# A hybrid decoder layer on eight cores: a build-time list scheduler for every engine, GpSimd arithmetic on VectorE, GLU gates ahead of values

## The chip, the cores and the metric

The kernel runs on one Trainium2 chip, on all 8 of its cores (two dies, cores 0 to 3 and 4 to 7). Each core takes half of one prompt (1024 tokens and 128 tokens of history) and four of the 32 sample tokens; no core talks to another. The time is device time of the slowest core, in microseconds (us). Each run lists every core's span and the mean TensorE clock that it was granted. In some executions a die is slow, at a lower clock; such runs are called slow and are not used for verdicts. A milder form stays inside runs called fast: two cores of a die have a clock that is about 0.02 lower and are some 10 to 25 us longer.

Engines: PE is TensorE (PEld its weight loads), DVE is VectorE, ACT is ScalarE, POOL is GpSimd, SP only issues transfers. POOL issues transfers too. Each engine is given one list of instructions; what it means that a list is worked through in order shows in e1, where VectorE stood 32.87 us before one copy.

## The reference, cut to what matters

```python
h = rms_norm(x, norm_mix_g)
z = h @ w_in                       # q | k | v | GLU value | GLU gate
q = rope(rms_norm(q, q_norm_g), pos);  k = rope(rms_norm(k, k_norm_g), pos)
a = attn_prompt(q, k, v, sinks)    # band of 128 keys; attn_sample reads cache_k, cache_v
u = u_val * jax.nn.sigmoid(u_gate)
c, new_c = causal_dwconv(u, c_buf, conv_w, conv_b)         # 31 taps per channel
c = jax.nn.silu(layer_norm(c, conv_ln_g, conv_ln_b))
x = x + jnp.concatenate([a, c], axis=-1) @ w_out
hm = rms_norm(x, norm_mlp_g)
x = x + jnp.square(jax.nn.relu(hm @ w_up)) @ w_down
```

Width 2048, 16 query heads and 4 key heads of 64, 1024 convolution channels, MLP width 8192. Besides `x`, the new keys, values and convolution rows are outputs; most of the sample caches' new content is a shifted copy of the old.

## The kernel before: the parts that matter

The program is first recorded as a list of instructions with their reads and writes, which gives each its dependencies, and then replayed: each engine runs *its own list in the order in which it was recorded*, waiting on semaphores.

```python
def add(self, eng, fn, reads=(), writes=(), key=None, ...):
    ...                      # dependencies from the bytes read and written
    for bk in banks:         # one more rule: engines that touch a PSUM bank keep their order
        for e2, it in self.bank_last[bk].items():
            if e2 != eng:
                ins.deps.add(it)
    self.streams[eng].append(ins)
```

Stage one loads x in 16 chunks, scales each to bf16 on VectorE, squares it on ScalarE, sums the squares on GpSimd, and multiplies by the K/V weights:

```python
for kc in range(16):
    xd.append(dma("sp", xs_(), R(xt_d[kc]), ...))           # four buffers
    dma("pool", WKV(kc), ..., after=[xd[kc - 3]] if kc >= 3 else [])
    ...                                                     # small tables at kc 5 and 8
    ts("dve", HT(kc), xs_(), G1(kc), ALU.mult)
    act(SQX[kc % 2](), xs_(), AF.Square)                    # at kc 0 into SS1
    if kc >= 2:
        tt("pool", SS1(), SS1(), SQX[(kc - 1) % 2](), ALU.add)
    ...                                                     # K/V matmuls of 7 tiles
for kc in range(16):
    dma("pool", WQ(kc), ..., after=[xd[15]] if kc >= 2 else [xd[13]])
```

The norm and rotary of Q and K go through ScalarE, VectorE and GpSimd.

```python
def qk_chain(accv, nh, nt, GC, GS, tix, B_, out_bf, ...):
    act(B_.SQ(hs), accv(hs), AF.Square)                     # reads the PSUM bank
    tt("dve", A(hs), accv(hs), bc(GC(tix)), ALU.mult)       # same bank
    ...                                                     # two half-head products into B
    red(ss(hs), B_.SQ(hs))
    act(rs(hs), ss(hs), AF.Ln, ...); act(rs(hs), rs(hs), AF.Exp, scale=-0.5)
    tt("pool", A(hs), A(hs), B_.B(hs), ALU.add)
    tt("pool", out_bf, A(hs), rsb, ALU.mult)
```

After Q come cache copies and loads, then GLU, convolution and attention interleaved by hand. The convolution needs u shifted by partitions, 16 small SP copies per channel block (`u_done`). After the last block the program reloads x (`xt_load`) and starts the output projection.

```python
dma("sp", R(nks[:, 0:127, :]), R(ck[:, 1:128, :]), "d2d", ...)   # and nvs, ncs: DRAM to DRAM
dma("pool", KTS(...), R(ckt), "cks", ...)                        # old keys, old values
dma("pool", CVB(p=(0, 127)), R(cv...), "cks", ...)
...
for pi in range(3):
    for gate in (True, False):
        u_job(c, pi, wg if gate else wv, gate)
...
def down_group(g, wd, last):          # MLP, after up_group(g + 1)
    for dc in range(16):
        ...
        tt("dve", x3(), accb((0, 3), (0, PW)), x3(), ALU.add)
```

Names: WKV, WQ, wu, wo, wup and wdn are the weights of K/V, Q, the GLU, the output projection and the MLP's two halves; ckt and cv are the old keys and values of the sample caches; nks, nvs and ncs are the new caches; u is the output of the GLU.

Of the kernel before, what the change touches and what calls it, by code (L numbers as in the profile page):

```python
# [31 lines left out]
NO = 1028  # L32
# [8 lines left out]
NKV1 = 7  # L41
# [6 lines left out]
class Ins:  # L48
    __slots__ = ("eng", "fn", "deps", "inc", "count", "key", "is_dma", "group", "name")

    def __init__(self, eng, fn, name=""):
        self.eng = eng
        self.fn = fn
        self.deps = set()
        self.inc = False
        self.count = 0
        self.key = None
        self.is_dma = False
        self.group = False
        self.name = name  # L60

# [88 lines left out]
class Prog:  # L150
    ENGS = ["pe", "act", "dve", "pool", "sp"]

    def __init__(self):
        self.streams = {e: [] for e in self.ENGS}
        self.spaces = {"sb": Space(), "ps": Space()}
        self.finals = []
        self.keycount = {}
        self.bank_last = {}
        self.n = 0

    def add(self, eng, fn, reads=(), writes=(), key=None, group=False, final=False, name="", after=(), claim=()):
# [34 lines left out]
        for ref in claim:  # L196
            for (sp, a, b) in ref.rngs:
                for st in self.spaces[sp].segs(a, b):
                    st[0] = ins
                    st[1] = []  # L200
        if key is not None:
            ins.is_dma = True
            ins.key = key
            ins.group = group
            self.keycount[key] = self.keycount.get(key, 0) + 16
            ins.count = self.keycount[key]
            ins.inc = True
# [4 lines left out]
        return ins  # L212

# [82 lines left out]
def build_program():  # L296
# [138 lines left out]

    def dma(eng, out, in_, key, group=False, final=False, after=()):
        return P.add(eng, lambda e: e.dma_start(out=out.ap, in_=in_.ap), reads=[in_], writes=[out],  # L437
                     key=key, group=group, final=final, after=after)

    def act(out, in_, func, bias=0.0, scale=1.0):  # L440
        rd = [in_]
        b = bias
        s = scale
        if isinstance(bias, Ref):
            rd.append(bias)
            b = bias.ap
        if isinstance(scale, Ref):
            rd.append(scale)
            s = scale.ap
        return P.add("act", lambda e: e.activation(out=out.ap, in_=in_.ap, func=func, bias=b, scale=s),  # L450
                     reads=rd, writes=[out])

    def tt(eng, out, in0, in1, op):
        return P.add(eng, lambda e: e.tensor_tensor(out=out.ap, in0=in0.ap, in1=in1.ap, op=op),  # L454
                     reads=[in0, in1], writes=[out])

    def ts(eng, out, in0, s1, op0, s2=None, op1=None):
# [5 lines left out]
        if isinstance(s2, Ref):  # L463
# [4 lines left out]
                     reads=rd, writes=[out])  # L468

    def cp(eng, out, in_):  # L470
        if eng == "act":
            return P.add("act", lambda e: e.copy(out=out.ap, in_=in_.ap), reads=[in_], writes=[out])  # L472
        return P.add(eng, lambda e: e.tensor_copy(out=out.ap, in_=in_.ap), reads=[in_], writes=[out])  # L473

    def red(out, in_):
        return P.add("dve", lambda e: e.tensor_reduce(out=out.ap, in_=in_.ap, axis=AX.X, op=ALU.add),  # L476
                     reads=[in_], writes=[out])

    def memset(eng, out, val):
        return P.add(eng, lambda e: e.memset(out.ap, val), writes=[out])  # L480

    def mm(out, lhsT, rhs, start, stop):
        return P.add("pe", lambda e: e.matmul(out.ap, lhsT.ap, rhs.ap, start=start, stop=stop),  # L483
                     reads=[lhsT, rhs], writes=[out])

    def tr(out, in_, ident):
        return P.add("pe", lambda e: e.transpose(out.ap, in_.ap, ident.ap), reads=[in_, ident], writes=[out])  # L487
# [34 lines left out]
    for kc in range(16):  # L522
        xs_ = XST[kc % 4]
        xd.append(dma("sp", xs_(), R(xt_d[kc]), "xst%d" % (kc % 4)))
        dma("pool", WKV(kc), R(wkv_d[kc]), "wkv%d" % kc, after=[xd[kc - 3]] if kc >= 3 else [])
# [10 lines left out]
        if kc >= 2:  # L536
            tt("pool", SS1(), SS1(), SQX[(kc - 1) % 2](), ALU.add)
# [3 lines left out]
    tt("pool", SS1(), SS1(), SQX[1](), ALU.add)  # L541
# [6 lines left out]
    def kv_tile(ti, bk):  # L548
        tn, c0, nt = TT[ti]
        for kc in range(16):  # L550
# [3 lines left out]
    kv_tile(7, 0)  # L554
    ptk = ps_f32(7, 1, (10,))
    for ti, (tn, c0, nt) in enumerate(TT):
# [5 lines left out]
    kv_tile(8, 1)  # L562
    kv_tile(9, 2)
    RB = sb(O_X, F32, (NU,))
    for i, (a, b) in enumerate(PU):
        pb = ps_f32(6 - i, 1, (b - a,))
        mm(pb(), ONF(), SS1((U0 + a, U0 + b)), True, True)
# [3 lines left out]
    cp("pool", IDB(), CST((0, 128)))  # L571
    cp("pool", MOWN(), CST((128, 256)))
    cp("pool", MPRV(), CST((256, 384)))
    cp("pool", MPR0(), CST((384, 512)))
    cp("pool", I4(), CST((512, 544)))
    for (GC, GS, g, gs) in ((GCK, GSK, GK, GKS), (GCQ, GSQ, GQ, GQS)):
        tt("pool", GC(), TABIN(0), bc(g, 1, (128, 10, 64)), ALU.mult)
        tt("pool", GS(), TABIN(1), bc(gs, 1, (128, 10, 64)), ALU.mult)
# [15 lines left out]
    KC = [sb(O_H + 7168 + 1024 * i, F32, (4, 64)) for i in range(2)]  # L594
# [3 lines left out]
    def qk_chain(accv, nh, nt, GC, GS, tix, B_, out_bf, out_f32=None):  # L598
# [14 lines left out]
        tt("pool", A(hs, p=pp), A(hs, p=pp), B_.B(hs, p=pp), ALU.add)  # L613
        rsb = bc(rs(hs, p=pp), 2, (nt, nh, 64))
        if out_f32 is not None:
            tt("pool", out_f32, A(hs, p=pp), rsb, ALU.mult)
            cp("pool", out_bf, out_f32)
        else:
            tt("pool", out_bf, A(hs, p=pp), rsb, ALU.mult)
# [5 lines left out]
    for ti, (tn, c0, nt) in enumerate(TT):  # L625
# [11 lines left out]
        kf = head4(KF_L, nt) if tn == "m7" else (head4(KF_S, nt) if tn == "s" else KC[ti % 2](p=pp))  # L637
        qk_chain(RAW[ti], 4, nt, GCK, GSK, ti, kb_, K2[ti](p=pp), out_f32=kf)

    def fin_k(tis, bk):  # L640
        pt = ps_bf16(bk, (4, 2, 128))
        for i, ti in enumerate(tis):
# [17 lines left out]
    def fin_q(qbuf, ti, c0d, nt):  # L660
        pt = ps_bf16(6 + ti % 2, (8, 128))
        qf = Buf("sb", qbuf.ap.rearrange("p h d -> p (h d)"), qbuf.off, (1024,), 2)
# [18 lines left out]
    for kc in range(16):  # L681
        for i in range(3):
# [11 lines left out]
    for i, ti in enumerate(range(4, 10)):  # L694
        for kc in range(16):
# [27 lines left out]
    GT = [sb(O_H + 4096 + 1440 * i, F32, (360,)) for i in range(2)]  # L723
    SGR = [sb(O_H + 6976 + 1440 * i, F32, (360,)) for i in range(2)]
# [14 lines left out]
    later = []  # L739

    def flush():
        while later:
            later.pop(0)()

    def u_job(c, pi, w, gate):
        a, b = PU[pi]
        n = b - a
        acc = dense_bank(n)
        for kc in range(16):
            mm(acc(), w(kc), HT(kc, (U0 + a, U0 + b)), kc == 0, kc == 15)  # L750
        flush()
        i = gts[0] % 2
        if gate:
            gt, sg = GT[i]((0, n)), SGR[i]((0, n))
            rb = RB((a, b))
# [4 lines left out]
            tt("pool", sg, gt, rb, ALU.mult)  # L760
        else:
            sg = SGR[i]((0, n))
            tt("dve", UB[c % 2]((a, b)), acc(), sg, ALU.mult)
            if pi == 2:
                tt("dve", UF(c), acc((322, 356)), SGR[i]((322, 356)), ALU.mult)
            gts[0] += 1

    def u_done(c):
        ub, u4 = UB[c % 2], U4[c % 2]
        first = None  # L770
        for s in range(4):
            for g in range(4):
# [5 lines left out]
                      key="u4%d" % (c % 2))  # L778
        cw4 = PAR((568 + 32 * c, 600 + 32 * c))
        tt("pool", D4[c % 2](), Ref(I4().ap.unsqueeze(1).unsqueeze(1).broadcast_to([128, 4, 8, 32]), I4().rngs),  # L780
# [8 lines left out]
    def conv_job(c, pi):  # L789
        acc = dense_bank(512)  # L790
        for t in range(8):
# [3 lines left out]
        flush()  # L795
        act(CC(c, (512 * pi, 512 * pi + 512)), acc(), AF.Identity, bias=CB(c))

    def conv_sums(c, eng="pool"):
# [10 lines left out]
    def unit_a(ui):  # L809
        n, gp = units[ui]  # L810
        own_c0 = MC0 + 128 * n
        cs = (gp * 4, gp * 4 + 4)
        for kb in range(2):
# [12 lines left out]
    def unit_b(ui):  # L826
# [3 lines left out]
        psd = ps_f32(5, 1, (4, 128))  # L830
        for kb in range(2):
# [12 lines left out]
        later.append(lambda: tt("dve", AT(cs, (128 * n, 128 * n + 128)), pso(), rec(), ALU.mult))  # L844

    def sample_a():
        ktn = KT((0, 2), (SC0, SC0 + SPC))
        cp("dve", Ref(KTS.ap[:, :, :, 127], KTS().rngs), Ref(ktn.ap.rearrange("p c s -> p s c"), ktn.rngs))
        pss2 = [ps_f32(0, 1, (64,)), ps_f32(1, 1, (64,))]
# [12 lines left out]
    def sample_b():  # L862
        psos = ps_f32(4, 1, (8, SPC))
        psds = ps_f32(5, 1, (8, SPC))
        for s in range(SPC):
# [9 lines left out]
        later.append(lambda: tt("dve", AT((0, 8), (1024, NO)), psos(), RECS(), ALU.mult))  # L875
# [10 lines left out]
    for c in range(8):  # L886
        wg, wv = wu.pop(0), wu.pop(0)
        for pi in range(3):
            for gate in (True, False):
                u_job(c, pi, wg if gate else wv, gate)  # L890
                if c == 0 and pi == 0 and gate:
                    while pend:
                        fin_q(*pend.pop(0))
                if job % 3 == 1 and nu < 16:
                    if nu >= 1:
                        unit_b(nu - 1)
                    unit_a(nu)
                    nu += 1
                if c == 4 and pi == 0 and not gate:
                    sample_a()  # L900
                if c == 4 and pi == 1 and not gate:
                    sample_b()
                job += 1
            if c >= 2 and pi < 2:
                conv_job(c - 2, pi)
                if pi == 1:
# [18 lines left out]
    def wo_half(dc, half, src):  # L925
# [3 lines left out]
        accb = acc3(next_slot())  # L929
        for kc in range(8):  # L930
# [13 lines left out]
    def ln_stats():  # L944
        for pi, (a, b) in enumerate(PM):
            pm, pv = ps_f32(6, 1, (PW,)), ps_f32(7, 1, (PW,))
# [36 lines left out]
    def norm2(dc):  # L983
# [3 lines left out]
        if dc == 0:  # L987
            cp("pool", SS(), sq())
        else:
            tt("pool" if dc < 14 else "dve", SS(), SS(), sq(), ALU.add)  # L990
# [7 lines left out]
    def norm2_end():  # L998
        for pi, (a, b) in enumerate(PM):
            pm = ps_f32(6 + pi % 2, 1, (PW,))  # L1000
# [17 lines left out]
    def up_group(g):  # L1018
        hid = HID[g % 2]
        for fi in range(GFF):  # L1020
            w = upq.pop(0)
            accb = acc3(next_slot())
            for kc in range(16):
# [11 lines left out]
    def down_group(g, wd, last):  # L1035
        hid = HID[g % 2]
        for dc in range(16):
            accb = acc3(next_slot())
            for fi in range(GFF):
# [14 lines left out]

    P.finish()
# [147 lines left out]
```

## Time and profile before

| | before |
|---|---|
| time, median of 6 runs | 1454.25 us (1452.68 to 1463.55) |
| span of the profiled core | 1451.3 us |
| PE busy | 1322.7 us (91%) |
| DVE / ACT / POOL busy | 694.6 / 285.8 / 312.3 us |

The chain of waits that ended last, by engine (part 4 of the page), says that the matter is TensorE:

```profile
PE 81%; DVE 6%; issue 4%; ACT 4%; DMA 2%; POOL 1%; SPq 1%; DVEq 0%; ACTq 0%; POOLq 0%
```

So the question is where PE is not busy. Busy time by stretch; the columns are the stretch and its length, then PE, PEld, DVE, ACT and POOL busy with the number of instructions, the granted clock, the DMA share and GB/s (a packet counts where it starts, so that a short stretch can show a share over 1):

```profile
0.00:62.00 62.00, 33.75 (x116) 11.94 (x117) 48.94 (x23) 21.58 (x20) 51.61 (x35) 0.89 0.83 210
62.00:106.00 44.00, 36.02 (x188) 17.72 (x185) 24.31 (x49) 20.44 (x58) 36.72 (x61) 0.95 0.72 114
106.00:168.00 62.00, 52.38 (x283) 25.22 (x284) 29.81 (x34) 21.18 (x38) 43.66 (x20) 0.91 0.33 63
168.00:371.00 203.00, 171.12 (x1399) 90.42 (x1396) 84.12 (x180) 99.22 (x186) 72.24 (x62) 0.96 0.44 76
371.00:387.00 16.00, 4.89 (x44) 1.81 (x48) 4.87 (x10) 3.01 (x4) 0.00 (x0) 0.62 0.99 188
387.00:550.00 163.00, 153.12 (x1037) 99.31 (x1030) 71.97 (x65) 57.52 (x57) 46.07 (x37) 0.96 0.59 109
550.00:1437.00 887.00, 870.93 (x5957) 580.29 (x5956) 429.16 (x377) 62.84 (x61) 61.99 (x117) 1.00 0.47 79
```

The first number after the length is PE: 28 us idle in stage one, 8 and 10 in the Q stages, 32 in the GLU stage, 11 in the short stretch after 371 us, 10 in the projection, and 16 in the MLP.

The price of GpSimd arithmetic is in the groups by shape (count, busy us, mean ns of one, idle before):

```profile
L454 POOL TENSOR_TENSOR arena<-arena 128x1032 f32<-128x1032 f32 x23 | 54.5, 2377 | 22.1 <-ACT arena L450 17.4 <-PE psum L483 4.7
L454 DVE TENSOR_TENSOR arena<-arena 128x1032 f32<-128x1032 f32 x22 | 26.9, 1229 | 21.6 <-ACT arena L450 20.7 <-DVE arena L454 0.2
```

And from the timeline of stage one (start, duration, instruction, idle before):

```profile
16.17 43.40 DVE L467 TENSOR_SCALAR arena<-arena 128x1160 bf16<-128x1160 f32 x13 [1.02 <-DMA arena<-xt]
17.87 0.82 POOL L437 DMA_DIRECT2D arena<-wkv  x1
18.71 2.64 POOL L454 TENSOR_TENSOR arena<-arena 128x1160 f32<-128x1160 f32 x1
```

Thirteen scalings take 43.40 us, 3.3 us each; the first two of the kernel, with POOL quiet, took 0.82 us. The POOL rows repeat every 3.4 us.

SP's timeline shows when transfers were issued. The last 16 copies of u are issued between 371.20 and 382.07 us, and the reloads of x follow them:

```profile
25.57 20.73 SPq L437 DMA_DIRECT2D arena<-xt  x7
102.55 16.28 SPq L437 DMA_DIRECT2D nks<-ck  x1
371.20 10.87 SPq L776 DMA_DIRECT2D arena<-arena  x16
383.01 14.48 SPq L437 DMA_DIRECT2D arena<-xt  x16
```

### The profile page before, as it was taken

To read this page: it belongs to the slowest core of one execution; us is meant where nothing else is said; L and a number is where in the kernel's file an instruction comes from. 1 tells how busy PE (TensorE), PEld (TensorE's weight loads), DVE (VectorE), ACT (ScalarE), POOL (GpSimd) and SP (SyncE) were. 2 spreads that over 40 slices of the span, in tenths; PEclk is the share of its full clock that TensorE was granted. 3 is DMA by queue.
4 is the path that set the end of the run, shared out by engine and by line. 5 is a ranking of instruction groups with operands and counts; after the bars stand their busy time and mean duration, and the time that the engine had idled before them with its cause. 6 is when DMAs were issued, how large, how long until landed. Compare 5 with 4: busy or idle time off the path is not lost.

```text
span 1451.3 us, 22465 instructions; the slowest of 8 cores (1445.6 to 1451.3 us)
## 1 busy us (share of the span) xinstructions
PE 1322.7 (91%) x9016; PEld 826.8 (57%) x9016; DVE 694.6 (48%) x734; ACT 285.8 (20%) x424; POOL 312.3 (22%) x330
## 2 busy tenths in 40 slices
PE   4779788788699979999999999999999999999996
PEld 1334344444366646666666666666666666666664
DVE  6765343343374322544534535535446345354364
ACT  3253345445233621000010010000100100100000
POOL 7976523333202712010010010110100100101000
PEclk8999899999799999999999999999999999999998
DMA  9764254354875358471562543634715526437209
GB/s 255 144 111 87 12 101 81 60 98 80 195 160 74 44 88 140 65 116 30 88 94 47 94 71 61 102 50 67 117 30 88 88 45 100 66 59 124 44 15 218
DMA packets 57336, 130.96 MB, mean 90 GB/s; under 512 B 19064, under 2 KB 22012, under 8 KB 57212
## 3 DMA queue, kind: packets, MB, share of 16 engines
q0 software_dynamic: 38880, 90.74, 40.5%
q1 hardware_dynamic: 18356, 38.80, 9.9%
q8 instruction: 73, 1.20, 0.3%
q14 instruction: 27, 0.22, 0.1%
HBM read 202.73 MB, written 10.35 MB: 147 GB/s over the span
## 4 chain that ended last, share of the span: by engine, by line
PE 81%; DVE 6%; issue 4%; ACT 4%; DMA 2%; POOL 1%; SPq 1%; DVEq 0%; ACTq 0%; POOLq 0%
PE psum L483 81%; DVE arena L454 4%; ACT arena L450 3%; DVE arena L467 2%; DMA arena<-xt 1%; POOL arena L454 1%; SPq L776 1%; DMA arena<-wup 0%; ACT arena L472 0%; DMA arena<-arena 0%; DVE arena L476 0%; PE psum L487 0%; SPq L437 0%; DVEq L265 0%; DVE arena L473 0%
## 5 line engine op out<-in xcount | busy, mean ns | idle before, releaser
L483 PE MATMUL psum<-arena 128*128 128x344 bf16 (+7 forms) x8924 | 1317.5, 323 | 103.8 <-DVE arena L454 38.1
L483 PEld LDWEIGHTS psum<-arena 128*128 128x128 bf16 (+4 forms) x8924 | 821.1, 99 | 596.8 <-issue 170.9
L454 DVE TENSOR_TENSOR arena<-psum,arena 128x1032 f32<-128x1032 f32 (+7 forms) x408 | 423.0, 1050 | 291.8 <-PE psum L483 264.7
L454 DVE TENSOR_TENSOR arena<-arena 128x1032 bf16<-128x1032 bf16 (+6 forms) x252 | 204.7, 824 | 427.1 <-ACT arena L450 410.3
L450 ACT ACTIVATE arena<-psum 128x512 bf16<-128x512 f32 (+6 forms) x150 | 112.5, 787 | 808.9 <-PE psum L483 797.9
L454 POOL TENSOR_TENSOR arena<-arena 128x1032 f32<-128x1032 f32 (+8 forms) x112 | 191.2, 1719 | 174.6 <-ACT arena L450 145.3
L437 POOL DMA_DIRECT2D arena<-wup x64 | 34.0, 531 | 746.1 <-PE psum L483 746.0
L450 ACT ACTIVATE arena<-arena 128x352 f32<-128x352 f32 (+11 forms) x237 | 148.9, 647 | 219.1 <-DVE arena L454 134.4
L467 DVE TENSOR_SCALAR arena<-arena 128x1160 bf16<-128x1160 f32 (+2 forms) x25 | 49.2, 2006 | 12.4 <-DMA arena<-xt 11.3
L437 POOL DMA_DIRECT2D arena<-wdn x64 | 34.0, 551 | 27.9 <-PE psum L483 25.8
L437 POOL DMA_DIRECT2D arena<-wo x16 | 11.6, 726 | 80.8 <-PE psum L483 80.8
L476 DVE TENSOR_REDUCE arena<-arena 128x4 f32<-128x256 bf16 (+4 forms) x27 | 17.2, 638 | 2.0 <-ACT arena L450 1.1
L450 ACT ACTIVATE arena<-psum,arena 128x512 f32<-128x512 f32 x16 | 11.1, 694 | 31.0 <-PE psum L483 31.0
L487 PE MATMUL psum<-arena 128*128 128x128 bf16 (+1 forms) x92 | 7.2, 220 | 10.9 <-DVE arena L454 5.6
L472 ACT COPY arena<-psum 128x1024 bf16<-128x1024 bf16 (+5 forms) x18 | 13.0, 762 | 15.4 <-PE psum L483 12.7
L487 PEld LDWEIGHTS psum<-arena 128*128 128x128 bf16 (+1 forms) x92 | 5.9, 101 | 13.6 <-issue 11.9
L437 POOL DMA_DIRECT2D arena<-wkv x16 | 12.3, 770 | 0.9 <-POOLq L297 0.9
L437 POOL DMA_DIRECT2D arena<-wu x16 | 9.0, 564 | 0.1
L437 POOL DMA_DIRECT2D arena<-wq x16 | 8.5, 599 | 0.0
L450 ACT ACT_TABLE_LOAD x3 | 3.8, 1283 | 21.2 <-PE psum L483 11.2
L473 DVE COPY arena<-psum 128x512 f32<-128x512 f32 (+1 forms) x8 | 4.7, 621 | 4.2 <-PE psum L483 4.2
L473 POOL CAST arena<-arena 128x256 bf16<-128x256 f32 (+3 forms) x15 | 5.2, 398 | 1.3
(11 smaller groups left out, 11.8 us busy)
## 6 DMA issues: line engine op xcount, KB each, us to landing
arena<-wup POOLq DMA_DIRECT2D x64, 512.0 KB, 6.8
arena<-wdn POOLq DMA_DIRECT2D x64, 512.0 KB, 14.5
arena<-xt SPq DMA_DIRECT2D x16, 580.0 KB, 7.7
arena<-arena SPq DMA_DIRECT2D x128, 65.8 KB, 4.5
arena<-xt SPq DMA_DIRECT2D x16, 516.0 KB, 13.6
yt<-arena SPq DMA_DIRECT2D x16, 514.0 KB, 8.8
arena<-wu POOLq DMA_DIRECT2D x16, 512.0 KB, 9.0
arena<-wo POOLq DMA_DIRECT2D x16, 512.0 KB, 8.1
```

Source lines behind the costliest of these rows:

```text
L437: return P.add(eng, lambda e: e.dma_start(out=out.ap, in_=in_.ap), reads=[in_], writes=[out], key=key, group=group, final=final, after=after)
L450: return P.add("act", lambda e: e.activation(out=out.ap, in_=in_.ap, func=func, bias=b, scale=s), reads=rd, writes=[out])
L454: return P.add(eng, lambda e: e.tensor_tensor(out=out.ap, in0=in0.ap, in1=in1.ap, op=op), reads=[in0, in1], writes=[out])
L467: return P.add(eng, lambda e: e.tensor_scalar(out=out.ap, in0=in0.ap, scalar1=a, scalar2=b, op0=op0, **kw), reads=rd, writes=[out])
L472: return P.add("act", lambda e: e.copy(out=out.ap, in_=in_.ap), reads=[in_], writes=[out])
L473: return P.add(eng, lambda e: e.tensor_copy(out=out.ap, in_=in_.ap), reads=[in_], writes=[out])
L476: return P.add("dve", lambda e: e.tensor_reduce(out=out.ap, in_=in_.ap, axis=AX.X, op=ALU.add), reads=[in_], writes=[out])
L483: return P.add("pe", lambda e: e.matmul(out.ap, lhsT.ap, rhs.ap, start=start, stop=stop), reads=[lhsT, rhs], writes=[out])
L487: return P.add("pe", lambda e: e.transpose(out.ap, in_.ap, ident.ap), reads=[in_, ident], writes=[out])
L776: P.add("sp", (lambda src=src, dst=dst: (lambda e: e.dma_start(out=dst.ap, in_=src.ap)))(), reads=[src], writes=[u4()] if i == 0 else [], ...
```

## The change

The intent: a static program order leaves engines standing behind an instruction that is not ready while a later one is. So the builder simulates the machine with a cost for every instruction, and gives each engine its list in the order of modelled readiness (lowest program index first among those ready). Besides, GpSimd does no arithmetic any more, the three GLU gates of a block come before its three values, and eight K/V tiles instead of seven are multiplied in stage one. Smaller parts of the change: keys that are not an output are written to bf16 at once, without an f32 copy; the gates have four buffers; and the last multiplication of an attention unit is no longer deferred by hand. The core of the diff:

```diff
-NKV1 = 7
+NKV1 = 8
+    LAT = {"pe": 200, "act": 110, "dve": 110, "pool": 150}
+    DMA_NS = 2000
+    DMA_RATE = 290.0
+    def schedule(self):
+        ...                                   # units: PE groups, else single instructions
+        for i in order:
+            ins = units[i][0]
+            if ins.is_dma:                    # only transfers of the same key keep their order
+                if ins.key in lastkey:
+                    users[lastkey[ins.key]].append((i, 1))
+                    ndep[i] += 1
+                lastkey[ins.key] = i
+        ...
+        while events:
+            ...
+            for e in self.ENGS:               # all five, SP and POOL too
+                if free[e] > now or not ready[e]:
+                    continue
+                _, i = heapq.heappop(ready[e])     # lowest program index that is ready
+                ...
+                if u[0].is_dma:
+                    st = max(end, dma_free)
+                    dma_free = st + u[0].nbytes / self.DMA_RATE
+                    fin = dma_free + self.DMA_NS
...
-        dma("pool", WKV(kc), R(wkv_d[kc]), "wkv%d" % kc, after=[xd[kc - 3]] if kc >= 3 else [])
+        dma("pool", WKV(kc), R(wkv_d[kc]), "wkv%d" % kc, after=[xd[kc - 2]] if kc >= 2 else [])
-            tt("pool", SS1(), SS1(), SQX[(kc - 1) % 2](), ALU.add)
+            tt("dve", SS1(), SS1(), SQX[(kc - 1) % 2](), ALU.add)
...                                            # likewise the chain ends, gate scale, tap matrices, LayerNorm and norm sums
-        for pi in range(3):
-            for gate in (True, False):
-                u_job(c, pi, wg if gate else wv, gate)
+        for step, (gate, pi) in enumerate(((True, 0), (True, 1), (True, 2), (False, 0), (False, 1), (False, 2))):
+            u_job(c, pi, wg if gate else wv, gate)
...
+    P.schedule()
     P.finish()
```

## The prediction

> **What bounds the kernel now.** TensorE is busy 1322.7 of 1451.3 us (page, part 1) and holds 81% of the chain that ended last. PE busy by stage (busy time in given stretches):
>
> - 0 to 62 us, x and K/V: 33.8 (DVE 48.9, POOL 51.6)
> - 62 to 106, K chains, three Q tiles: 36.0 of 44
> - 106 to 168, rest of Q: 52.4 of 62
> - 168 to 371, GLU, convolution, attention: 171.1 of 203
> - 371 to 387, waiting for shifted copies of u: 4.9 of 16
> - 387 to 550, output projection: 153.1 of 163
> - 550 to 1437, MLP: 870.9 of 887, clock 1.00
> - tail: 14 us of evictions and stores
>
> MLP and tail are full or DMA-bound; I expect nothing there. All must come from the first 550 us, where PE idles about 99 us.
>
> **What the change does, costed.**
>
> 1. GpSimd arithmetic to VectorE. A 128x1032 f32 add takes 2.38 us on POOL, 1.23 on DVE (groups by shape), ratio 1.93; [...] a 128x1160 scaling takes 0.82 us with POOL quiet, about 3.4 next to a POOL add. Stage one runs at POOL's period (0.82 issue + 2.64 add = 3.46 us x 16 = 55 us). On DVE: 0.82 + about 1.4 = 2.2 us x 16 = 35 us, below the DMA (12.7 MB at about 285 GB/s, 45 us). The WQ loads, issued at 62 us because POOL is behind, come about 13 us earlier. Eight K/V tiles instead of seven: 3.4 us less PE afterwards. Cost: DVE needs about 6 us per Q tile, under PE's 7.4; in the GLU stage DVE goes from about 42% to 65% busy.
> 2. K chains (in series, 77 to 103 us) and Q chains overlap; Q tile 4 starts near 86 instead of 106. The hole after the last Q tile (153 to 168) shrinks to about 8 us. Items 1 and 2 together: GLU starts about 26 us earlier.
> 3. GLU stage: 32 us of PE idle from gate chains and attention exponentials in fixed order. Gates first, order by readiness: about 15. Gain 16.
> 4. At 371 us SP issues 16 copies (10 us) plus 4.9 us landing while PE waits. The projection's attention half needs none of this and can go first. Gain 9.
> 5. At 510 us PE waits 7 us for wup, whose issue sat behind POOL adds. Gain 7.
>
> Sum 58 us, nearly all on PE's path; early loads of x (2.1 MB) compete with WQ (about 5 us, counted in 2), and a static order from modelled times will be wrong in places.
>
> **Prediction: 1396 us, 8 in 10 between 1372 and 1426. Faster by over 2%: 0.88; within 2%: 0.09; slower: 0.03.**
>
> **What would show it.** 1: DVE scaling at 0.8 to 1 us, no POOL arithmetic, last K/V step near 50 us. 2: steady GLU matmuls by 142 us. 3: GLU stage near 187 us long, PE over 90% busy. 4: no PE wait for u copies over 3 us; projection matmuls before the last convolution. 5: no wait for wup. MLP within 5 us of before.
>
> **What would make it wrong.** DVE, carrying everything in order, makes TensorE wait for evictions in Q or GLU (PE waits for DVE grow); early prefetches delay WQ or the u copies; the modelled order puts a late instruction ahead of a ready one; more than three activation table loads.

The sum came to 58 us (26 + 16 + 9 + 7). The ratio of 1.93 and the scaling times next to it are from the trace. Where other figures of item 1 can be read, all in the profile of the kernel before: the DMA engines moved 284 GB/s from 10 to 20 us, at a share of 0.98; the "about 1.4" is an estimate, the 1.23 us of DVE's add taken from 1032 to 1160 columns; the 32 matmuls of 512 columns of a Q tile took 7.07 us at a clock of 1.00, so that 16 come to 3.5 us (I wrote 3.4). Of "full or DMA-bound", the first half is the MLP (PE busy 870.9 of 887 us), the second the tail, with a DMA share of 0.84 from 1437 to 1451 us. The 5 us for the early loads of x were my estimate, for which I gave no derivation.

## More of the kernel before

One piece of the MLP, where an up projection ends and a down projection begins (weight loads and POOL left out):

```profile
579.04 1.03 ACT L450 ACTIVATE arena<-psum 128x1032 bf16<-128x1032 f32 x1 [5.97 <-PE psum L483]
580.17 2.03 DVE L454 TENSOR_TENSOR arena<-arena 128x1032 bf16<-128x1032 bf16 x2 [4.97 <-ACT arena L450]
582.12 2.37 DVE L454 TENSOR_TENSOR arena<-psum,arena 128x1032 f32<-128x1032 f32 x2
583.50 0.74 PE L483 MATMUL psum<-arena 128*128 128x344 bf16 x4 [1.05 <-DVE arena L454]
```

VectorE does two multiplications of the hidden tile (2.03 us) and only then the residual add that frees PSUM; PE waits 1.05 us.

## The result

The changed kernel takes 1435.91 us (median of 10 runs, 1434.21 to 1507.87) against 1455.56 us before (20 runs). The ratio of fast runs is 0.9857, 95% interval 0.9837 to 0.9877: 1.4% faster, where 4% was forecast. The ratios are those on record for the fast runs; they are not quite the ratios of the medians.

| | before | after |
|---|---|---|
| span of the profiled core | 1451.3 us | 1434.7 us |
| PE busy | 1322.7 us | 1317.7 us |
| DVE / ACT / POOL busy | 694.6 / 285.8 / 312.3 us | 739.2 / 279.9 / 112.0 us |

The moments at which stages end tell more. They are read from the records of each core, and the table gives the median over the eight cores of the profiled run, in us from the core's first instruction. "GLU in motion" is the end of the 33rd GLU matmul (two jobs done); the projection ends with the 768th matmul of 344 columns. A few matmul records can be missing, which moves such an end by some tenths.

| | last x scaling | last WQ landed | last Q matmul | GLU in motion | last GLU matmul | projection ends | MLP ends | span |
|---|---|---|---|---|---|---|---|---|
| before | 60 | 92 | 153 | 172 | 367 | 510 | 1435 | 1450 |
| after | 75 | 136 | 188 | 212 | 369 | 513 | 1419 | 1429 |

By differences of neighbouring columns: the start until the last Q matmul became 35 us *longer*, the hole to the GLU stage 5 longer (19 to 24), the GLU stage 38 shorter (195 to 157), the rest up to the projection's end 1 longer, the MLP 19 shorter (925 to 906), the tail 5 shorter. The sum is the 21 us by which the span fell. (Why the tail is shorter was not looked into; in the runs below it varies between 10 and 17 us.)

Busy time by stretch, first the GLU stage of the kernel before between the same two moments, then the changed kernel (same columns as above):

```profile
172.00:367.00 195.00, 165.38 (x1357) 88.01 (x1360) 80.23 (x173) 97.07 (x183) 68.04 (x57) 0.97 0.45 79
```

```profile
0.00:75.00 75.00, 31.19 (x112) 11.33 (x113) 34.77 (x37) 20.98 (x23) 13.97 (x27) 0.84 0.86 211
75.00:136.00 61.00, 35.93 (x154) 16.08 (x155) 23.71 (x70) 17.28 (x56) 12.49 (x17) 0.78 0.96 138
188.00:212.00 24.00, 14.06 (x89) 6.53 (x88) 21.15 (x30) 12.28 (x25) 0.12 (x1) 0.79 0.00 1
212.00:369.00 157.00, 156.40 (x1332) 86.61 (x1331) 99.18 (x208) 88.45 (x175) 9.04 (x16) 1.00 0.54 100
369.00:403.00 34.00, 20.71 (x181) 12.29 (x178) 13.67 (x18) 5.01 (x7) 2.10 (x3) 0.89 1.05 224
```

The GLU stage is now full: PE is busy 156.40 of 157 us, where before it was busy 165.38 of 195. So 29 of the 38 us are idle time that went, and 9 are busy time for about the same matmuls. The clock, 1.00 instead of 0.97, would account for about 5 of these (an estimate: 3% of 165 us). But in the early stages PE idles 44 us in the first 75 and 25 in the next 61, with the DMA engines at 0.86 and 0.96. What they carry is in the issue timelines. SP:

```profile
7.12 0.83 SPq L562 DMA_DIRECT2D nks<-ck  x1
8.01 0.65 SPq L562 DMA_DIRECT2D nvs<-cv  x1
8.70 0.61 SPq L562 DMA_DIRECT2D ncs<-sc  x1
9.89 55.88 SPq L562 DMA_DIRECT2D arena<-xt  x12
```

POOL:

```profile
2.78 1.08 POOL L562 DMA_DIRECT2D arena<-wu  x2
73.26 0.90 POOL L562 DMA_DIRECT2D arena<-ckt  x1 [2.41 <-ACT arena L575]
74.14 4.85 POOL L562 DMA_DIRECT2D arena<-cv  x1
78.98 7.45 POOL L562 DMA_DIRECT2D arena<-wq  x14
```

The DRAM copies, issued at 102 to 120 us before, now go out at 7 to 9 us, ahead of the fifth chunk of x; the first GLU weights go out at 2.8 us; and the two cache loads slip between the second and the third WQ load. All are transfers that depend on little and are needed late. VectorE shows the first effect (one scaling of 0.82 us, after a wait of 15.80 us for x), and the list of waits the second (waiter, releaser, us in total, times, longest):

```profile
46.91 0.82 DVE L592 TENSOR_SCALAR arena<-arena 128x1160 bf16<-128x1160 f32 x1 [15.80 <-DMA arena<-xt]
```

```profile
PE psum L615 <- DMA arena<-wq: 25.0, 2, 24.7
PE psum L615 <- DMA arena<-arena: 14.6, 2, 13.2
```

The last line is mostly the wait for the shifted copies of u. It differs much between cores: of all waits of this kind around the end of the GLU stage, the cores have 2.1 to 14.6 us (median 9.0), against 7.9 to 10.8 us (median 9.9) before. In the timeline, six reloads of x are issued just ahead of the last 16 copies, and PE starts the convolution only at 404.32 us:

```profile
364.28 8.05 SPq L562 DMA_DIRECT2D arena<-xt  x6
373.24 12.20 SPq L909 DMA_DIRECT2D arena<-arena  x16
404.32 5.95 PE L615 MATMUL psum<-arena 128*32 128x512 bf16 x60 [13.19 <-DMA arena<-arena]
```

And the same piece of the MLP as above: the residual add (1.23 us from PSUM) now stands between the two multiplications, and PE waits 0.27 us.

```profile
577.11 1.03 ACT L575 ACTIVATE arena<-psum 128x1032 bf16<-128x1032 f32 x1 [5.97 <-PE psum L615]
578.25 0.70 DVE L579 TENSOR_TENSOR arena<-arena 128x1032 bf16<-128x1032 bf16 x1 [4.97 <-ACT arena L575]
578.87 1.23 DVE L579 TENSOR_TENSOR arena<-psum,arena 128x1032 f32<-128x1032 f32 x1
580.02 1.22 DVE L579 TENSOR_TENSOR arena<-arena 128x1032 bf16<-128x1032 bf16 x1
582.53 0.74 PE L615 MATMUL psum<-arena 128*128 128x344 bf16 x4 [0.27 <-DVE arena L579]
```

### The profile page after: what moved, and what is told of

Its sections match the earlier page's. It is cut to its first block, busy times and chain, and to the rows that moved or that the text cites. A ratio compares the mean times of both kernels' runs of the same rounds, so it can differ in the third digit from the quotient of the medians.

```text
span 1434.7 us, 22372 instructions; the slowest of 8 cores (1419.6 to 1434.7 us)
## 1 busy us (share of the span) xinstructions
PE 1317.7 (92%) x9016; PEld 826.1 (58%) x9016; DVE 739.2 (52%) x851; ACT 279.9 (20%) x429; POOL 112.0 (8%) x200
## 4 chain that ended last, share of the span: by engine, by line
PE 84%; DMA 9%; DVE 3%; issue 1%; ACT 1%; SPq 1%; POOL 1%; DVEq 0%; ACTq 0%; POOLq 0%
PE psum L615 83%; DMA arena<-xt 4%; DMA arena<-wq 3%; DVE arena L579 3%; DMA arena<-arena 1%; ACT arena L575 1%; SPq L909 1%; POOL arena L562 1%; PE psum L619 0%; DVE arena L592 0%; ACT L575 0%; DVEq L374 0%; ACT arena L597 0%; SPq L562 0%; ACTq L374 0%
## 5 line engine op out<-in xcount | busy, mean ns | idle before, releaser
L615 PE MATMUL psum<-arena 128*128 128x344 bf16 (+5 forms) x8924 | 1313.2, 322 | 104.9 <-DMA arena<-wq 25.0
L615 PEld LDWEIGHTS psum<-arena 128*128 128x128 bf16 (+2 forms) x8924 | 820.4, 99 | 591.6 <-issue 168.7
L579 DVE TENSOR_TENSOR arena<-psum,arena 128x1032 f32<-128x1032 f32 (+8 forms) x408 | 426.3, 1050 | 242.7 <-PE psum L615 193.0
L579 DVE TENSOR_TENSOR arena<-arena 128x1032 bf16<-128x1032 bf16 (+11 forms) x364 | 287.3, 806 | 406.2 <-ACT arena L575 387.8
L575 ACT ACTIVATE arena<-psum 128x512 bf16<-128x512 f32 (+7 forms) x150 | 115.9, 786 | 805.7 <-PE psum L615 804.7
L592 DVE TENSOR_SCALAR arena<-arena 128x1160 bf16<-128x1160 f32 (+2 forms) x25 | 15.7, 626 | 31.0 <-DMA arena<-xt 30.1
L562 POOL DMA_DIRECT2D arena<-cv x1 | 4.8, 4850 | 0.0
```

The source lines that it names most:

```text
L562: return P.add(eng, lambda e: e.dma_start(out=out.ap, in_=in_.ap), reads=[in_], writes=[out], key=key, group=group, final=final, after=aft ...
L575: return P.add("act", lambda e: e.activation(out=out.ap, in_=in_.ap, func=func, bias=b, scale=s), reads=rd, writes=[out], cost=cost("act", ...
L579: return P.add(eng, lambda e: e.tensor_tensor(out=out.ap, in0=in0.ap, in1=in1.ap, op=op), reads=[in0, in1], writes=[out], cost=cost(eng, o ...
L592: return P.add(eng, lambda e: e.tensor_scalar(out=out.ap, in0=in0.ap, scalar1=a, scalar2=b, op0=op0, **kw), reads=rd, writes=[out], cost=c ...
L615: return P.add("pe", lambda e: e.matmul(out.ap, lhsT.ap, rhs.ap, start=start, stop=stop), reads=[lhsT, rhs], writes=[out], cost=c)
```

## The experiments

Theories. A: the scheduler also orders SP and POOL, and hoists transfers that nobody needs soon; these delay x, WQ and the copies of u. B: VectorE has too much work since the move. C: the compute order by modelled times is bad. All runs gave correct results. On four chips the kernel before had medians of 1462.53 (e1 to e4), 1462.91 (e5 to e8), 1460.16 (e9 to e12) and 1455.31 us (e13, e14), so compare ratios. The stages of all runs, as in the table above (the expectations often quote the profiled core of the changed kernel, with its last scaling at 71 and WQ at 129 us; the medians of the eight cores are 75 and 136):

| run | ratio to before (95%) | last x | WQ | last Q | GLU in motion | last GLU | projection ends | MLP ends | span |
|---|---|---|---|---|---|---|---|---|---|
| e1_fifo | 0.9613 (0.9594 to 0.9631) | 52 | 79 | 167 | 190 | 347 | 482 | 1388 | 1401 |
| e2_nosched | 1.0092 (1.0046 to 1.0139) | 53 | 80 | 148 | 167 | 378 | 531 | 1451 | 1466 |
| e3_pool_back | 0.9765 (0.970 to 0.983) | 84 | 122 | 183 | 206 | 368 | 499 | 1404 | 1417 |
| e4_gates_back | 0.9841 (0.9824 to 0.9858) | 75 | 135 | 187 | 211 | 367 | 514 | 1420 | 1432 |
| e5_hold_cache | 0.9602 (0.9576 to 0.9628) | 75 | 107 | 160 | 184 | 341 | 484 | 1389 | 1402 |
| e6_hold_d2d | 0.9771 (0.9688 to 0.9854) | 60 | 121 | 173 | 197 | 354 | 495 | 1401 | 1414 |
| e7_hold_wu | 0.9819 (0.9765 to 0.9873) | 70 | 128 | 182 | 206 | 363 | 507 | 1413 | 1425 |
| e8_hold_all | 0.9637 (0.9609 to 0.9665) | 53 | 83 | 138 | 161 | 330 | 470 | 1374 | 1385 |
| e9_hold_copy | 0.9524 (0.9494 to 0.9554) | 54 | 85 | 137 | 160 | 323 | 459 | 1364 | 1379 |
| e10_u_first | 0.9486 (0.9442 to 0.953) | 55 | 85 | 138 | 161 | 323 | 458 | 1364 | 1378 |
| e11_best_pool | 0.9593 (0.955 to 0.9635) | 65 | 95 | 154 | 177 | 344 | 475 | 1380 | 1393 |
| e12_fifo_copy | 0.9470 (0.9443 to 0.9497) | 54 | 82 | 138 | 160 | 318 | 456 | 1360 | 1378 |
| e13_mlp_swap | 0.9916 (0.9901 to 0.9931) | 60 | 92 | 152 | 172 | 367 | 511 | 1425 | 1438 |
| e14_square2 | 0.9428 (0.9412 to 0.9445) | 53 | 80 | 138 | 152 | 310 | 447 | 1353 | 1366 |

### e1: transfers in program order

```diff
             if ins.is_dma:
-                if ins.key in lastkey: ...
+            if ins.eng in ("sp", "pool"):        # each of the two queues keeps program order
+                if ins.eng in lastkey: ...
```

> The changed kernel, but the scheduler keeps the DMA issues of SP and of POOL in program order; TensorE, ScalarE and VectorE are still reordered. Theory A (the scheduler hoists transfers that nobody needs soon, and these delay x, WQ and the u copies): last x scaling at 50 to 55 us instead of 71, WQ landed by 85 us instead of 129, GLU matmuls steady by about 145 us instead of 211; total near 1370 us. Theory B (VectorE is overloaded by the GpSimd arithmetic): total unchanged, 1430 to 1440. Theory C (the compute order is what is wrong): unchanged, 1425 to 1440.

The early stages came as theory A said: last scaling 52, WQ at 79. The time fell to a ratio of 0.9613. But the GLU was in motion only at 190 us, not by 145, and the total, 1406 us, stayed 36 us above what A expected. The timeline shows a new wait:

```profile
133.98 0.19 DVE L599 COPY arena<-arena 128x8 bf16<-128x8 bf16 x1 [32.87 <-DMA arena<-cv]
136.58 1.01 PE L619 MATMUL psum<-arena 128*128 128x128 bf16 x8 [29.33 <-DVE arena L579]
```

A copy of eight columns, the new key into the cache tile, needed only by the sample attention in the fifth GLU block, stands in VectorE's list in the middle of the Q chains. It waits 32.87 us for the cache load, and the Q chains behind it wait too, PE 29.33 us. The scheduler put it there: its model counts about 4 us for that load (2 us plus 0.5 MB at 290 bytes per ns, the size at four bytes an element); it landed 61.0 us after its issue here, 43.1 in the changed kernel and 29.7 in the kernel before. From 101.11 us, the end of its last addition, until 133.98 us VectorE started nothing, in front of this one copy. So A is right but not whole, and a fourth theory, A2, is: the model's short transfer times put a waiting instruction ahead of ready ones.

### e2: no scheduler

```diff
-    P.schedule()
```

> The changed kernel without the call of the scheduler: all engines in program order, GpSimd arithmetic on VectorE, gates ahead. Theory A: DMA order is that of before, so x and WQ arrive early (last scaling at 50 to 55 us, WQ by 85), but the waits of the GLU stage come back; total 1400 to 1425, below the changed kernel. Theory B: slower than before or equal, 1450 or more. Theory C (the scheduler's compute order loses): clearly faster than the changed kernel, at or below 1390.

The early stages are good (53, 80, last Q at 148), so the DMA order was indeed the scheduler's doing. But the GLU stage takes 211 us (167 to 378), more even than the 195 before, and the total is 0.9% *slower* than before; A's 1400 to 1425 was too low. The move to VectorE and the new GLU order alone are worth nothing. What gains is the order of TensorE, ScalarE and VectorE: e1, with the transfers in the same order, is at 0.9613. Theory C has lost. (The kernel before deferred the last multiplication of each attention unit by hand; that device is gone from the changed program, which may be why its plain order is the slower one. This was not tried. In the GLU stage PE waits 21.1 us for ScalarE here, on core 0, against 6.1 us in the profile of before.)

### e3: GpSimd arithmetic back, all else as changed

```diff
-            tt("dve", SS1(), SS1(), SQX[(kc - 1) % 2](), ALU.add)
+            tt("pool", SS1(), SS1(), SQX[(kc - 1) % 2](), ALU.add)     # and all the others
```

> The changed kernel with the GpSimd arithmetic put back on GpSimd (norm sums, Q/K chain ends, gate times 1/rms, tap matrices, LayerNorm sums); scheduler and gates ahead stay. Theory A: early stages are DMA-bound anyway, so about the same start of the GLU stage (205 to 225 us), and the GLU stage somewhat longer; total 1435 to 1455. Theory B: faster than the changed kernel, below 1425, with the GLU stage starting before 190 us.

This was a surprise: median span 1417 against 1429 us. By the number of the profiled run (1421.11, below 1425) it spoke for theory B, but its GLU stage starts at 206, not before 190. The table says where the 12 us come from: the GLU is in motion 6 us earlier, the GLU stage is 5 us longer (162 against 157), and the stretch from there to the projection's end is 13 us shorter (131 against 144). The first part is the order of transfers again: with POOL busy, the two cache loads are issued at 111 and 113 us, *behind* all WQ and the first GLU weight loads instead of at 73 and 74 ahead of most WQ loads, and WQ lands at 122 instead of 136. In the last part no core of this run waits for the copies of u (median 9.0 us in the changed kernel): three reloads of x go out just ahead of the last 16 copies, not six. So e3 says nothing for theory B; it moved transfers too. The interval is wide because two fast runs near 1421 us and one at 1439 with two low-clock core pairs are averaged. A clean test of the move has to have its transfers in order: that is e11.

### e4: gates and values in turn again

```diff
-((True, 0), (True, 1), (True, 2), (False, 0), (False, 1), (False, 2))
+((True, 0), (False, 0), (True, 1), (False, 1), (True, 2), (False, 2))
```

> The changed kernel with gate and value of the same columns next to each other again in program order; scheduler and VectorE stay. The changed kernel's GLU stage is about 160 us against 203 before. If the gates ahead make most of that, this one loses 15 us or more (1450 or more); if the order by readiness alone makes it, under 5 us (1434 to 1440).

The GLU stage is 156 us against 157, the ratio 0.9841 against 0.9857: the gates ahead are worth nothing that can be measured once a scheduler orders the engines.

### e5 to e7: one hoisted transfer held at a time

e5 holds the two cache loads, e6 the DRAM copies, e7 the first GLU weights:

```diff
+    hold = [P.streams["pe"][-1]]       # PE's last instruction so far: the Q stage
-    dma("pool", KTS((0, SPC), (0, 2), (0, 127)), R(ckt), "cks", group=True)
+    dma("pool", KTS((0, SPC), (0, 2), (0, 127)), R(ckt), "cks", group=True, after=hold)   # e5; also cv
-    dma("sp", R(nks[:, 0:127, :]), R(ck[:, 1:128, :]), "d2d", ...)
+    dma("sp", R(nks[:, 0:127, :]), R(ck[:, 1:128, :]), "d2d", ..., after=hold)            # e6; also nvs, ncs
-    wu = [wstream(wu_d[order[i]], "wu", 128) for i in range(4)]
+    wu = [wstream(wu_d[order[i]], "wu", 128, after=[last_wq]) for i in range(4)]          # e7
```

> The changed kernel, with only the two GpSimd-queue cache loads (ckt, cv; issued at 73 us, between the second and third WQ load) made to wait for TensorE's last Q-stage instruction so far in program order. If these two loads are what delays WQ (landed at 129 us, 46 us median from issue), WQ lands by 105 and GLU starts by about 185 instead of 211: total 1405 to 1415. If the early reloads of x and wu or VectorE are to blame, WQ lands after 120 and the total stays within 1428 to 1438.

> The changed kernel, with only the three DRAM-to-DRAM cache copies (issued at 7 to 9 us, ahead of the fifth x chunk) held until TensorE's Q stage. If they cause the stall of x (15.8 us without an x chunk, last scaling at 71 us), the last scaling comes at 58 to 62 us and the total falls by about 10 us, 1422 to 1428. If not, within 4 us of the changed kernel.

> The changed kernel, with only the first four GLU weight loads (two of which issue at 3 us, 1 MB read each) held until the last WQ load has landed. If they share the blame for the stall of x, the last scaling comes 5 to 8 us earlier, 63 to 66 us, total 1425 to 1432; if not, no change.

The cache loads (e5) and the DRAM copies (e6) hit, both with more than expected in the span; e7 is a hit in the stages only, since its median of 1435.69 us and its interval, which contains the 0.9857 of the changed kernel, don't show a gain. Holding the cache loads brings WQ from 136 to 107 and the median span from 1429 to 1402 us (27 us). Holding the DRAM copies brings the last scaling from 75 to 60 and the span to 1414 (15 us). Holding the GLU weights brings it to 70 and the span to 1425 (4 us). The fast runs of e6 and e7 are of two kinds, near 1420 and 1438, and near 1430 and 1442; the higher ones have two cores at a clock of about 0.955. That is why I use the spans.

### e8 and e9: all held; and the small copy held

e8 is e5, e6 and e7 together, and the first four reloads of x held to the second GLU block. e9 also holds the copy found in e1:

```diff
-        cp("dve", <new key column of KTS>, <KT>)
+        cp("dve", <new key column of KTS>, <KT>, [P.streams["pe"][-1]])   # when PE reaches the sample attention
```

> All holds together: cache copies, cache loads, first GLU weights, and the first four reloads of x (held until the second GLU block). TensorE, ScalarE and VectorE orders are nearly those of the changed kernel. Theory A: last x scaling near 52 us, WQ by 85, GLU steady by about 145 instead of 211, GLU stage still about 160 us: total near 1366 (1355 to 1385). If GLU start stays after 180, theory A has lost.

> All holds of the previous run, and the small VectorE copy of the new key column into the cache tile (it waits for the ckt and cv loads) made to wait until TensorE reaches the sample attention. In the run before, VectorE, in order, stood 12.4 us in front of this copy and the next Q and GLU work waited behind it. Theory A2 (the scheduler's short transfer times put a waiting instruction ahead of ready ones on an in-order engine): that wait is gone, undisturbed cores fall from 1380-1385 us to about 1366-1372. If the wait only moves elsewhere: unchanged.

e8: scalings done at 53, WQ at 83, last Q matmul at 138, span 1385: theory A holds in the early stages, and the three gains of e5 to e7 add up (27, 15 and 4 make 46, and e8 has 44, with the reloads of x held besides). By the ratio, 0.9637, e8 looks no better than e5; both its fast runs have two cores at a clock of about 0.965, so the span is the better measure here. But GLU is in motion at 161, not 145, so 1366 was missed: the hole after Q has not shrunk. e9 takes 6 us more off the span (1379; expected about 14): the wait of 12.4 us before the copy stood in the GLU stage and was partly hidden (on core 2 of both runs, PE's longest wait for VectorE falls from 10.0 to 0.8 us; the stage is 163 us instead of 169).

In the profiled run of e8 the lower clock held two cores of a die and not the others. Busy time from 75 to 150 us, cores 0 and 2 of the same die (core 1 has 0.81 there too, core 3 has 0.97); the clock is the third number from the right:

```profile
75.00:150.00 75.00, 72.30 (x326) 31.81 (x325) 45.38 (x61) 19.46 (x39) 3.43 (x7) 0.81 0.27 46
75.00:150.00 75.00, 65.66 (x349) 30.90 (x352) 56.27 (x76) 26.37 (x55) 7.72 (x7) 0.95 0.39 63
```

### e10: copies of u before the reloads of x

```diff
-        xt_load(dc, [c1_pe] if dc < 4 else [])
+        xt_load(dc, [c1_pe] if dc < 4 else [u4_last])
```

> The run e9, and the reloads of x from the fifth on wait for the last shifted copy of u. In the changed kernel six of them and two weight loads are issued ahead of the last 16 copies, which then take 19 us to land; TensorE waits 13.2 us. Expected: the copies land about 5 us after the last issue, TensorE waits under 4 us, and the LayerNorm stall after it (5.5 us) shrinks: undisturbed cores 8 to 14 us below e9. If the weight loads, not x, are what slows the copies: within 3 us of e9.

A miss. The copies now land 2.6 us after issue (median over all cores) instead of 9.2, and the last convolution ends at 342 instead of 348; but the projection ends at 458 instead of 459. There was little left to win: I had taken the 13.2 us from one core of the changed kernel, while in e9 PE waits only 1.0 to 4.9 us for the copies (median 2.4, and 0.4 in e10). The LayerNorm chain on VectorE takes part of that back: PE waits for VectorE 5.9 us on every core of e9, and 2.3 to 11.6 us (median 6.9) in e10. The profiled core of e10 has the longest such wait (waits of PE from 300 to 460 us):

```profile
PE psum L615 <- DVE arena L579: 11.6, 2, 11.2
PE psum L615 <- DMA arena<-arena: 0.9, 1, 0.9
```

I take it that there the attention half of the projection had been used up before the LayerNorm was done, so that nothing was left to hide it behind; no run tests this.

### e11: the move to VectorE by itself, with transfers in order

The edit of e3, on e10.

> The run e10 with the GpSimd arithmetic back on GpSimd. Once transfers are in good order, the start should be bound by GpSimd again (scalings at 3.4 us, last one near 60 instead of 52) and the GLU stage should be longer (175 instead of 160 us as in e3): 15 to 30 us slower than e10. Theory B (VectorE is overloaded by the move): equal to e10 or faster.

Last scaling at 65 instead of 55, last Q at 154 instead of 138, GLU stage 167 instead of 162; span 1393 against 1378. So the move is worth 15 us once transfers do not hide it, and theory B as a total has lost.

### e12: program order for transfers, and the one copy

The edits of e1 and of the copy in e9, nothing else.

> The run e1 (SP and GpSimd queues in program order) with only the one VectorE copy held. In e1 VectorE stood 32.9 us before this copy while TensorE waited 29.3 us. Theory A2: the 29 us come back, undisturbed cores from about 1399 to 1370. If another wait takes its place: above 1390.

The ratio is 0.9470, the cores' spans 1374 to 1381 us; 23 of the expected 29 us came back, and two small edits do as much as all the holds. What remains against my prediction is the hole from the last Q matmul to the GLU stage: 22 us (138 to 160).

### e13: one instruction pair in the MLP of the kernel before

```diff
-            tt("dve", hid(fi), hid(fi), RS2f(), ALU.mult)
+            if fi < GFF - 1:
+                tt("dve", hid(fi), hid(fi), RS2f(), ALU.mult)
+            else:                                 # after the next group's first residual add
+                late.append(lambda: tt("dve", hid(GFF - 1), hid(GFF - 1), RS2f(), ALU.mult))
```

> The kernel before, unchanged but for one pair of VectorE instructions per MLP group: the multiplication by 1/rms of the group's fourth hidden tile comes after the first residual add of the next down projection instead of ahead of it. In the trace of before TensorE waits 1.05 us for VectorE once per group, 15 waits and 16.1 us between 560 and 1400 us; in the changed kernel 17 waits and 4.5 us. If this order is what made the MLP shorter, the MLP waits fall to about 0.3 us each and the time falls by 11 to 12 us (ratio to before 0.992). If these are gaps of the record and not real, ratio 1.000 within 0.002.

A hit: ratio 0.9916, 0.9901 to 0.9931, which is 12 us. PE's waits for VectorE between 560 and 1400 us, first in the kernel before, then in this one:

```profile
PE psum L483 <- DVE arena L454: 16.1, 15, 1.3
```

```profile
PE psum L483 <- DVE arena L454: 4.1, 15, 0.4
```

So the gap was real and not a lack in the records, and this one order is 12 of the 19 us that the MLP became shorter. The other 7 fit the wait for wup (6.3 us of waiting in the profile of before; in the table it falls after the projection's last matmul), which neither the changed kernel nor e2 has.

### e14: a second buffer for the squares of Q

```diff
+    qb.SQB = sb(O_E, BF16, (16, 64))       # a raw K/V tile that is dead by then
-        act(B_.SQ(hs, p=pp), accv(hs, p=pp), AF.Square)
+        SQ = B_.SQB if nh == 16 and i % 2 else B_.SQ
+        act(SQ(hs, p=pp), accv(hs, p=pp), AF.Square)
```

On e12.

> The run e12 with a second buffer for the squares of Q (taken from a raw K/V tile that is dead by then). In e12 the Q chains run about two tiles behind TensorE: the square of a tile waits for the reduction of the tile before it, and the other VectorE reads of the same bank wait for the square, so every tile takes 7.3 us where VectorE has 6.15 us of work. With two buffers VectorE should catch up while TensorE multiplies: the hole from the last Q matmul to the thirty-third GLU matmul shrinks from 22 us to about 14, total 5 to 9 us below e12. If VectorE's work itself sets the pace (theory B, overload by the move), the hole stays at 20 or more.

The hole shrinks to 14 us as expected, the span from 1378 to 1366 (12 us, more than the 5 to 9 expected; 8 are the hole and 4 the tail, not explained), the ratio to 0.9428: the best kernel, at 1371.28 us (median of four runs, 1370.16 to 1371.64, all fast). In e12 the timeline shows the chain at its slow pace. The lines are the copy of an earlier tile's transposed Q on ACT, the square of a tile (128x1024 from PSUM), and the first product of that tile on DVE, which the bank rule puts behind the square:

```profile
131.23 1.01 ACT L597 COPY arena<-psum 128x1024 bf16<-128x1024 bf16 x1 [5.12 <-PE psum L619]
132.34 1.01 ACT L575 ACTIVATE arena<-psum 128x1024 bf16<-128x1024 f32 x1
133.46 1.23 DVE L579 TENSOR_TENSOR arena<-psum,arena 128x1024 f32<-128x1024 f32 x1 [1.47 <-ACT arena L575]
136.94 1.21 DVE L603 TENSOR_REDUCE arena<-arena 128x16 f32<-128x1024 bf16 x1
```

In e12 the reductions of neighbouring tiles start 7.3 to 7.4 us apart (122.23, 129.65, 136.94); in e14 5.7 us apart (115.82, 121.54, 127.31) until they have caught up with PE. So VectorE's work did not set the pace of 7.3 us. But the trace of e12 shows another wait than the one that I expected: the reduction of the tile before ends at 130.86 us, and the square starts only after the copy, for which ACT has waited 5.12 us until PE, in its own list, came to the transposes. So the chains went at PE's pace (two tiles start 7.35 us apart there), a fixed distance behind it. With the second buffer the scheduler puts the square *ahead* of the copy (115.07 and 115.99 us in e14). The edit changed the buffer and, through the scheduler, this order; which of the two gained the 8 us was not separated.

## Why the prediction was wrong

The forecast was 1396 us with a range from 1372 to 1426 and a chance of 0.88 for more than 2%; measured was 1435.91, a ratio of 0.9857. Point by point:

1. **GpSimd to VectorE: right for the scalings, the effect hidden.** They do take 0.82 us (shown above for stage one), against 3.3 us next to POOL's additions; why they are slower there was not shown. "Last K/V step near 50 us" and WQ "about 13 us earlier" were right for a program whose transfers keep their order (e1: 52, and WQ 92 to 79). In the changed kernel they were 75 and 136. e11 puts the move's worth at 15 us.
2. **The step that failed: transfers that the scheduler moves were priced at "early loads of x (2.1 MB) compete with WQ (about 5 us, counted in 2)".** I had looked only at the one prefetch that came to mind. Hoisted were also the DRAM copies, two GLU weight loads and the cache loads, and they cost 15, 4 and 27 us (e6, e7, e5), 44 together (e8, which also holds the first reloads of x). The prediction names "early prefetches delay WQ or the u copies" among what would make it wrong, without looking for them in the diff, where they can be found: the scheduler treats SP and POOL like the other engines, and a transfer with no dependency is ready at time zero.
3. **"The hole after the last Q tile shrinks to about 8 us": wrong.** It went from 19 to 24 us, and is 22 in e12. I had compared VectorE's 6 us of work per tile with PE's 7.4 and not the chain: with one buffer of squares the scheduler's order held the chains at a fixed distance behind PE, and with two the hole is 14 us (e14).
4. **GLU stage: right in direction, mis-sized.** Expected was a gain of 16 us, measured 38 (195 to 157). PE is busy 156.40 of 157 us; I had left 15 us of idle that are not there, and had not counted that busy time falls too (165 to 156 us, with the clock at 1.00 instead of 0.97). The gain is the scheduler's (e2, 211 us without), hardly that of the gates ahead (e4).
5. **Copies of u, "gain 9": wrong in the changed kernel.** PE still waits for them, 9.0 us in the median of the cores against 9.9 before and 13.2 us at the longest, with reloads of x going out ahead of the copies, which land 11.6 us after issue instead of 5.3 (medians). The projection does come first, as I said. With transfers held, the wait is 2.4 us (e9), and the stretch from the last GLU matmul to the projection's end is 136 us against 143 before: most of the 9. Copies that land early are not enough by themselves, though: in e14 they land after 3.3 us, and PE still waits 2.4 to 11.6 us (median 7.4).
6. **wup, "gain 7": right.** The wait is gone.
7. **"MLP and tail are full; I expect nothing there": wrong by 12 us in the MLP.** The windows showed 16 us of idle there and the timeline 1.05 us per group, which I passed over. e13 shows that it was one order on VectorE.

The early stages lost 40 us (GLU in motion at 212 instead of 172), where I had promised 26 gained; the 38 in the GLU stage, 19 in the MLP and 5 in the tail paid for that and left 1.4%. That the total still fell is in part luck: the MLP's 12 us were not forecast at all. With transfers back in program order, one copy moved and one buffer added, the same scheduler gives 5.7% (e14).

What stays open: the early reloads of x were held only together with others, so their own cost was not measured; the eight K/V tiles were never tried by themselves; in e14, whether the buffer or the order that came with it gained; and why the plain order of the changed program is slower than that of before (e2).

## What to carry to other kernels

Let a scheduler order compute engines, but not transfers by readiness alone: here transfers with few dependencies went out at 2.8 us, at 7 to 9 us and at 73 to 74 us, ahead of chunks of x and WQ loads that were needed sooner, and cost 4, 15 and 27 us (e7, e6, e5). When you judge such a change, list for every transfer when its dependencies are met, and ask what it will then overtake. Where an engine works through its list in order, as VectorE did in e1, an instruction that waits for a transfer must stand late in the list: there the model counted about 4 us for a load that landed after 61.0 us, VectorE stood 32.87 us, and PE behind it 29.33 us. And a small gap that repeats once per loop in a trace (here 15 waits, 16.1 us, of which e13 won back 12) is to be explained before it is passed over.
